# One matmul of 512 columns in place of two of 256: image and context side by side in layer 0, high and low halves side by side in layer 1

## The chip, the cores and the metric

The kernel runs on 1 core of one Trainium2 chip. The metric is device time in microseconds (us): the median of three runs of the kernel before is 2149.61 us (2144.79 to 2152.18).

## What is computed

The reference is a network of two layers on an image stream `x` of 256 tokens and a context stream `ctx` of 256 tokens, each with 2048 features, in fp32. Cut to the parts that matter:

```
mod = silu(c) @ ada_w + ada_b;  h = rmsnorm(x) * (1 + scale) + shift         # for x and for ctx
layer 0:  p = h @ e_w_in   # q, k, v, gate, a/b and four more blocks of 2048 columns
          q,k,v = silu(conv3(...)); chunked gated delta rule over 16 heads, 2 directions
          y = concat(rmsnorm(o) * silu(z), b * conv3(c*h) * silu(z_b)) @ e_w_out;  x = x + gate * y
layer 1 (image only):  u, v = gelu(h @ W);  y_c = u * (w_s @ layernorm(v) + b_s) * silu(z_c)
          y_d = (mean_r(p_d) - p_d) @ pool_w * scale * silu(z_d)
          x = x + gate * (concat(y_c, y_d) @ o_w_out);  out = rmsnorm(x)
```

In layer 0 the context is needed only for keys, values and the a/b columns; queries and everything else are computed for the image alone.

## The kernel before

Every large product is made of three: both operands are split into a high part H (rounded to the matmul's fp32r type) and a low part L (the remainder), and H.H + H.L + L.H is accumulated in PSUM. A weight chunk of 128 x 1024 is loaded (`raw`), cast to H on ACT (line 202) and subtracted to L on DVE (line 209) by `wchunk`; there are four buffers of each. `proj` (line 218) then takes 128 x 128 pieces of H and L as the stationary operand and 256 tokens of activation as the moving one: for each piece the order is H with the high activation, H with the low one, L with the high one (line 230). With two streams (`acts` of length 2) each of these is issued twice, for the image into columns 0 to 255 and for the context into columns 256 to 511 of one PSUM bank. `projT_n` (lines 236 to 241) is the other form: activations stationary, 512 weight columns moving.

The stages, in the order of time:

- **Start, 0 to 220 us.** Modulation products (`ada_cols`, line 386), normed tokens transposed and split into `hxH`, `hxL` (image) and `hcH`, `hcL` (context) by `h_cols`, and between them, on 6 weight column blocks for each of 16 rows of blocks, `k_part` (line 450), whose sums go to six tiles `kacc`.
- **Keys and values, 220 to 480 us.** Ten steps of `proj` on `wkv` for both streams, each followed by `finish` (convolution, silu, transposes); `ab_proj` (line 504) and `ab_rows` make the gate rows.
- **Head groups, 480 to 1360 us.** Four groups of four heads. In each: `wq` and `wza` products, then a chain of small products (`G`, `Q`, `E`, `PT`, `XT`, `X`, then per chunk and direction `kS`, `QS`, `z`, `Sp`, `az`, at the end `oT`), and the `wbb` products, which stand between the steps of that chain on PE as far as they reach.
- **Out of layer 0 and into layer 1, to 1563 us.** `projT` on `wout0`, the norm, `projT` on `wv1` with `h1H`, `h1L` stationary.
- **Layer 1, 1563 to 1963 us.** For four groups: `proj` on `wpz` (p half), box means on DVE, `proj` on `wpz` (z half), `proj` on `poolw` with `y1H`, `y1L` moving; then 8 blocks of `proj` on `wuz` with gelu, tanh and the token mix (`sp`, line 1138). Two PSUM tiles `pj` of two banks alternate; each is read directly by ACT and DVE.
- **`wout1`, 1963 to 2147 us.** `projT` with `y1H`, `y1L` stationary.

The order on each engine is not written out: a list scheduler with its own timeline places the instructions, and each engine then runs its queue in order. A `pj` tile can be written again when its last reader on ACT or DVE is done.

Of the kernel before, what the change touches and what calls it, by code (L numbers as in the profile page):

```python
# [17 lines left out]
P = 128  # L18
# [52 lines left out]
def layout(a):  # L71
# [34 lines left out]
    u = o[:, :D].reshape(D, 8, 256)  # L106
    z = o[:, 2 * D:3 * D].reshape(D, 8, 256)
    r["wuz"] = _blk(np.stack([u, z], 2).reshape(D, 2 * D), 512)
    p = o[:, 3 * D:4 * D].reshape(D, 4, 512)
    z = o[:, 4 * D:5 * D].reshape(D, 4, 512)  # L110
    r["wpz"] = _blk(np.stack([p, z], 2).reshape(D, 2 * D), 512)
# [4 lines left out]
    r["poolw"] = f(a["o_pool_w"][0].reshape(4, 4, P, 512).transpose(0, 2, 1, 3)).reshape(4, P, D)  # L116
# [6 lines left out]
def body(ctx: ExitStack, tc: tile.TileContext, T, dbg=None):  # L123
# [92 lines left out]

    def proj(src, cols, acts, outs, shared, kts=KT):
        nk = 1024 // cols
        for c in range(kts // nk):
            H, L = wchunk(src[:, c * 1024:(c + 1) * 1024], nk)  # L220
            for kk in range(nk):
                k = c * nk + kk
                for n, o in enumerate(outs):
# [3 lines left out]
                    m = len(acts)  # L227
# [85 lines left out]
    hxH = hxp.tile([P, KT, 256], F32R, name="hxH")  # L313
    hxL = hxp.tile([P, KT, 256], F32R, name="hxL")
# [50 lines left out]
    with ExitStack() as ph1:  # L365
        hcp = pool("hc", stack=ph1)
        hcH = hcp.tile([P, KT, 256], F32R, name="hcH")
        hcL = hcp.tile([P, KT, 256], F32R, name="hcL")

        accp = pool("acc", stack=ph1)  # L370
        with ExitStack() as ph0:
# [6 lines left out]
            acc = [accp.tile([P, 2, 512], F32, name="kacc", tag=f"kacc{b}") for b in range(6)]  # L378
# [39 lines left out]
            def norm_tok(s):  # L418
                for n in (2 * s, 2 * s + 1):
                    junk = accp.tile([P, 2, 512], F32, name="junk", tag="kacc5")  # L420
# [9 lines left out]
            def h_cols(j, srcs=(0, 1)):  # L430
                tr = gp.tile([P, 4, P], F32, name="trp", tag="g")
                for s in srcs:
                    aH, aL = ((hxH, hxL), (hcH, hcL))[s]
# [51 lines left out]
            if "hT" in dbg:  # L485
                tap("hT", hcH.bitcast(F32))
# [4 lines left out]
        def row(name):  # L491
            return ap.tile([64, 512], F32, name=name)
# [712 lines left out]
```

## Time and profile before

| what | value |
|---|---|
| median of three runs | 2149.61 us |
| the profiled execution: its time | 2155.28 us |
| its span, first to last instruction | 2153.5 us |
| PE busy (matmuls, 17034) | 2069.5 us, 96% |
| DVE busy | 1526.0 us, 71% |
| ACT busy | 999.5 us, 46% |
| DMA queues' busiest | 61.8% of 16 engines |

Busy times of PE are of pipelined instructions with modelled ends: one matmul of 256 columns is listed with 284 ns, while the next starts 120 ns after it. What a matmul costs is therefore read from the starts of neighbours in the timeline, or from a run of equal matmuls in the chain of work, never from its listed duration. The 1.8 us between time and span lie outside the first and the last instruction.

### The profile page before, as it was taken

The page shows a single profiled execution, that of the slowest core. Times are in us where ns is not written, and L with a number is a line of the kernel's source. Part 1 is how long each engine was busy: PE and PEld are TensorE (multiplying, and loading weights), DVE is VectorE, ACT ScalarE, POOL GpSimd, SP SyncE. Part 2 cuts the span into 40 slices and gives each one's busy share as a digit, 9 for nine tenths or more (in the row PEclk, how much of TensorE's full clock was granted, in tenths as well). Part 3 has the DMA queues.
Part 4 walks back from the last instruction along what each step waited for, and adds up shares of the span by engine and source line. Part 5 has one row for each costly group of instructions (what it writes and reads, how often), then busy time and mean ns, then how long its engine had stood idle before and what let it go on. Part 6 is the DMA issues. An engine that isn't in the chain of part 4 may idle for free. (4 is left out here: it accounts for less than half of the span.)

```text
span 2153.5 us, 42176 instructions
## 1 busy us (share of the span) xinstructions
PE 2069.5 (96%) x17034; PEld 1928.5 (90%) x17034; DVE 1526.0 (71%) x2715; ACT 999.5 (46%) x1728; POOL 33.8 (2%) x51
## 2 busy tenths in 40 slices
PE   6999999999999999989999999898999999999997
PEld 4789999999989999989999878677899999998886
DVE  4447987877976898489758984788687676555554
ACT  5333365225554546445645554345454444444433
POOL 0000000000000000000000000000000000000000
PEclk9999999999999999999999999999999999999999
DMA  9777655776544775366448862797866666666664
GB/s 343 263 262 243 188 182 174 238 247 233 179 134 139 247 258 179 91 225 195 133 139 258 276 187 79 253 326 260 275 219 189 180 186 197 195 187 215 192 194 131
DMA packets 151267, 446.41 MB, mean 207 GB/s; under 512 B 16512, under 2 KB 23456, under 8 KB 150048
## 3 DMA queue, kind: packets, MB, share of 16 engines
q1 hardware_dynamic: 145936, 425.37, 61.8%
q0 software_dynamic: 5136, 18.35, 2.7%
q8 instruction: 133, 2.18, 0.4%
q14 instruction: 62, 0.51, 0.1%
HBM read 423.19 MB, written 20.46 MB: 206 GB/s over the span
## 5 line engine op out<-in xcount | busy, mean ns | idle before, releaser
L209 DVE TENSOR_TENSOR L<-raw,H 128x1024 fp32r<-128x1024 f32 (+1 forms) x554 | 667.6, 1208 | 374.8 <-ACT H L202 354.1
L202 ACT CAST H<-raw 128x1024 fp32r<-128x1024 f32 (+1 forms) x554 | 574.4, 1042 | 761.7 <-PE pj L230 419.4
L230 PE MATMUL pj<-hxH,H 128*128 128x256 f32 x1856 | 528.5, 285 | 4.2 <-DVE zb L946 4.2
L230 PE MATMUL pj<-hxH,L 128*128 128x256 f32 x1856 | 527.3, 284 | 0.0
L230 PE MATMUL pj<-hxL,H 128*128 128x256 f32 x1856 | 526.8, 284 | 0.0
L230 PEld LDWEIGHTS pj<-hxH,H 128*128 128x128 f32 x1856 | 352.4, 190 | 6.3 <-DVE zb L946 4.5
L230 PEld LDWEIGHTS pj<-hxH,L 128*128 128x128 f32 x1856 | 352.4, 190 | 2.4 <-issue 1.2
L230 PEld LDWEIGHTS pj<-hxL,H 128*128 128x128 f32 x1856 | 352.4, 190 | 1.0
L230 PE MATMUL pj<-h1H,H 128*128 128x256 f32 x1024 | 290.5, 284 | 0.0
L230 PE MATMUL pj<-h1H,L 128*128 128x256 f32 x1024 | 289.8, 283 | 0.0
L230 PE MATMUL pj<-h1L,H 128*128 128x256 f32 x1024 | 289.7, 283 | 0.0
L277 DVE SCALAR_TENSOR_TENSOR acc<-araw,cs,acc 128x512 f32<-128x512 f32 x240 | 178.9, 747 | 33.0 <-DMA araw<-in_ada 20.8
L230 PEld LDWEIGHTS pj<-h1H,H 128*128 128x128 f32 x1024 | 196.5, 192 | 0.2 <-issue 0.2
L230 PEld LDWEIGHTS pj<-h1L,H 128*128 128x128 f32 x1024 | 196.5, 192 | 0.0
L230 PEld LDWEIGHTS pj<-h1H,L 128*128 128x128 f32 x1024 | 196.5, 192 | 0.0
L230 PE MATMUL pj<-hcH,L 128*128 128x256 f32 x320 | 90.4, 283 | 0.0
L230 PE MATMUL pj<-hcH,H 128*128 128x256 f32 x320 | 90.4, 282 | 0.0
L230 PE MATMUL pj<-hcL,H 128*128 128x256 f32 x320 | 90.1, 281 | 0.0
L239 PE MATMUL pj<-H,y1H 128*128 128x512 f32 x192 | 76.0, 396 | 0.0
L241 PE MATMUL pj<-H,y1L 128*128 128x512 f32 x192 | 75.9, 396 | 0.0
L240 PE MATMUL pj<-L,y1H 128*128 128x512 f32 x192 | 75.9, 395 | 0.0
L230 PEld LDWEIGHTS pj<-hcH,L 128*128 128x128 f32 x320 | 60.1, 188 | 0.5 <-issue 0.4
(428 smaller groups left out, 3659.6 us busy)
## 6 DMA issues: line engine op xcount, KB each, us to landing
raw<-in_wbb SPq DMA_DIRECT2D x128, 512.0 KB, 3.8
raw<-in_wout SPq DMA_DIRECT2D x128, 512.0 KB, 4.0
araw<-in_ada SPq DMA_DIRECT2D x192, 256.0 KB, 4.5
raw<-in_ada SPq DMA_DIRECT2D x64, 512.0 KB, 6.5
raw<-in_wpz SPq DMA_DIRECT2D x64, 512.0 KB, 3.9
raw<-in_wuz SPq DMA_DIRECT2D x64, 512.0 KB, 3.6
raw<-in_wkv SPq DMA_DIRECT2D x40, 512.0 KB, 4.7
araw<-in_ada0g SPq DMA_DIRECT2D x64, 256.0 KB, 4.5
```

The source lines that it names most:

```text
L202: S.copy(H, raw)
L209: V.tensor_tensor(L, raw, H, ALU.subtract)
L230: PE.matmul(o[:, e * 256:(e + 1) * 256] if m > 1 else o, w, a[t][:, k, :], start=st and i == 0 and e == 0, stop=sp and i == 2, skip_group_ ...
L239: PE.matmul(o, xH[:, t], H[:, kk, :], start=st, stop=False, skip_group_check=True)
L240: PE.matmul(o, xH[:, t], L[:, kk, :], start=False, stop=False, skip_group_check=True)
L241: PE.matmul(o, xL[:, t], H[:, kk, :], start=False, stop=sp, skip_group_check=True)
L277: V.scalar_tensor_tensor(aacc[u // KT], raw, cs[:, k, 0:1], aacc[u // KT], ALU.mult, ALU.add)
```

## The change

- Layer 0: one tile `hxc` [128, stream, half, 16, 256] holds image and context, high and low. `k_part` (but for row 0), the `wkv` products and the a/b product use one matmul with a moving operand of two runs of 256 columns (image, context; 32 KB apart in a partition).
- The six accumulators, `wab` and two gate rows move into one tile `acc8`, which lies in the place of the later tile `hx`. When `acc8` is done with, 8 ACT copies of 128 x 1024 bring the image half from `hxc` to `hx` (line 634), since the head groups use 256 columns as before.
- Layer 1: `h1` and `y1` hold both halves in one tile. A new function `pair` multiplies each H piece with high and low activations as 512 columns (two runs of 256, 16 KB or 32 KB apart) and each L piece with the high activations as 256; the two sums stand side by side in PSUM. ACT copies the low one to SBUF (`jn`), DVE adds the high one (`join`). A `pair` covers two blocks of 128 weight columns where `proj` covered four, so `wpz`, `poolw` and `wuz` are cut into twice as many tiles of half the size; weight chunks are as many and as large as before.
- The software DMA scratch is halved to 2048 bytes per partition.

```diff
+    def both(t, k):
+        return hxc[:, :, t, k, :]
     def proj(src, cols, acts, outs, shared, kts=KT):
...
                     for i, (w, t) in enumerate(((wH, 0), (wH, 1), (wL, 0))):
-                        for e, a in enumerate(acts):
-                            PE.matmul(o[:, e * 256:(e + 1) * 256] if m > 1 else o, w, a[t][:, k, :],
-                                      start=st and i == 0 and e == 0, stop=sp and i == 2, skip_group_check=True)
+                        PE.matmul(o, w, acts(t, k),
+                                  start=st and i == 0, stop=sp and i == 2, skip_group_check=True)
...
-    hxH = hxp.tile([P, KT, 256], F32R, name="hxH")
-    hxL = hxp.tile([P, KT, 256], F32R, name="hxL")
+    acc8 = hxp.tile([P, 8, 2, 512], F32, name="acc8", tag="hx")
...
+        hxc = hxcp.tile([P, 2, 2, KT, 256], F32R, name="hxc")
...
-                        for q in srcs:
-                            a = ((hxH, hxL), (hcH, hcL))[q]
-                            PE.matmul(ps[n][:, q * 256:(q + 1) * 256], w_, a[t][:, j, :],
-                                      start=first and i == 0 and q == 0, stop=last and i == 2, skip_group_check=True)
+                        q = slice(srcs[0], srcs[-1] + 1)
+                        PE.matmul(ps[n].rearrange("p (s t) -> p s t", s=2)[:, q], w_, hxc[:, q, t, j, :],
+                                  start=first and i == 0 and srcs[0] == 0, stop=last and i == 2, skip_group_check=True)
...
+            if step > 6:
+                for t in range(2):
+                    for q in range(1 if step < 9 else 2):
+                        k4 = slice(4 * (step - 7 + q), 4 * (step - 6 + q))
+                        S.copy(hx[:, t, k4], hxc[:, 0, t, k4])
...
+    def pair(src, x, kts=KT):
+        ps = pj.tile([P, 2, 2, 256], F32, name="pj", tag="pj")
+        for c in range(kts // 4):
+            H, L = wchunk(src[:, c * 1024:(c + 1) * 1024], 4)
+            for kk in range(4):
+                k = c * 4 + kk
+                for n in range(2):
+                    w = slice(n * P, (n + 1) * P)
+                    PE.matmul(ps[:, n], H[:, kk, w], x[:, :, k, :], start=k == 0, stop=k == kts - 1,
+                              skip_group_check=True)
+                    PE.matmul(ps[:, n, 0], L[:, kk, w], x[:, 0, k, :], start=False, stop=k == kts - 1,
+                              skip_group_check=True)
+        t = Wk.tile([P, 2, 256], F32, name="jn", tag="jn")
+        S.copy(t, ps[:, :, 1])
+        return ps[:, :, 0], t
+    def join(ps, t):
+        V.tensor_tensor(t, t, ps, ALU.add)
+        return t
...
-        ps = pj.tile([P, 4, 256], F32, name="pj", tag="pj")
-        proj(T["wpz"][2 * g + 1], 512, [(hH, hL)], [ps[:, n, :] for n in range(4)], 2)
         zs = yo
-        silu_to(zs, ps)
+        for half in range(2):
+            t = join(*pair(T["wpz"][4 * g + 2 + half], h1))
+            silu_to(zs[:, 2 * half:2 * half + 2], t)
...
-    for blk in range(8):
-        ps = pj.tile([P, 4, 256], F32, name="pj", tag="pj")
-        proj(T["wuz"][blk], 512, [(hH, hL)], [ps[:, n, :] for n in range(4)], 2)
+    for gi in range(16):
+        uz = join(*pair(T["wuz"][gi], h1))
```

Three places in the instruction order. First ACT in the `wuz` stage of layer 1, before (`ug`, `zg`: gelu and tanh of one block of 256 columns; `H<-raw`: cast of one weight chunk):

```order
L1143 ACTIVATE ug<-pj 128x256
L1064 ACTIVATE zg<-pj 128x256
L202 CAST H<-raw 128x1024
L345 CAST y1H<-ug 128x256 x2
L202 CAST H<-raw 128x1024 x7
```

The same place now (`jn<-pj`: the copy of the low sum):

```order
L202 CAST H<-raw 128x1024 x2
L1087 COPY jn<-pj 128x512
L202 CAST H<-raw 128x1024
L1171 ACTIVATE jn<-jn 128x256
L1071 ACTIVATE zg<-jn 128x256
L202 CAST H<-raw 128x1024
L348 CAST y_15705<-jn 128x256
```

Where eight casts stood between two readings of PSUM there are four, and a copy stands ahead of gelu and tanh, which now read SBUF.

Second, ACT in the stage of keys and values, now (`ct`, `cth`: convolution and tanh; `ads`: a step of the modulation sums; the row of copies has no counterpart before):

```order
L202 CAST H<-raw 128x1024
L365 ACTIVATE cth<-ct 128x512
L634 COPY hx<-hxc 128x1024 x8
L289 COPY ads<-adc 128x128
L202 CAST H<-raw 128x1024 x2
L362 ACTIVATE ct<-pj,conv_123 128x512
```

The eight copies follow each other, ahead of the next two casts of weight chunks.

Third, PE at the end of the chain of head group 1 (the second of four), before (`pj` rows are products of `wbb` that stand between the steps):

```order
L230 MATMUL pj<-hxH,H 128x256
L898 MATMUL Sp<-zk,Kt 128x128 x3
L230 MATMUL pj<-hxL,H 128x256
L898 MATMUL Sp<-zk,Kt 128x128
L230 MATMUL pj<-hxH,L 128x256
L230 MATMUL pj<-hxH,H 128x256
L909 MATMUL az<-zs,aT 128x128 x4
L867 MATMUL kS<-St,KTt 128x128 x4
L875 MATMUL QS<-St,QT 128x128 x4
```

And now, from the place where the last `pj` row of the group has gone by (the steps that follow to `oT` go on in the same way, without a `pj` row):

```order
L905 MATMUL Sp<-zk,Kt 128x128
L874 MATMUL kS<-St,KTt 128x128 x4
L882 MATMUL QS<-St,QT 128x128 x4
L905 MATMUL Sp<-zk,Kt 128x128 x3
L894 MATMUL z<-r,U 128x128 x4
L905 MATMUL Sp<-zk,Kt 128x128 x4
L916 MATMUL az<-zs,aT 128x128 x4
```

Before, `pj` products stood between these steps up to the last but one; now they have been issued earlier (62 more of them between this group's `E` and its `PT`, 815 against 753), and the last four `z` steps follow each other bare, as they do in group 3 of either kernel.

## Rows read from the trace of the kernel before

**Rows 1.** The page: span, and busy time, share of the span and instructions of PE.

```profile
span 2153.5 us, 42176 instructions
PE 2069.5 (96%) x17034; PEld 1928.5 (90%) x17034; DVE 1526.0 (71%) x2715; ACT 999.5 (46%) x1728; POOL 33.8 (2%) x51
```

**Rows 2.** What PE waited for, longest first: total us, times, longest us.

```profile
PE adm L386 <- DMA raw<-in_ada: 18.4, 3, 16.5
PE oT L926 <- DVE on L923: 13.1, 2, 6.6
PE tr L1025 <- issue: 7.7, 1, 7.7
```

**Rows 3.** The chain of work that ended last, in the `wuz` stage: start us, us, what.

```profile
1890.75 0.89 PE sp L1138 x8
1891.64 23.04 PE pj L230 x192
1914.68 0.89 PE sp L1138 x8
```

**Rows 4.** The page's groups: count, busy us and mean ns of one, idle time before.

```profile
L209 DVE TENSOR_TENSOR L<-raw,H 128x1024 fp32r<-128x1024 f32 (+1 forms) x554 | 667.6, 1208 | 374.8 <-ACT H L202 354.1
L202 ACT CAST H<-raw 128x1024 fp32r<-128x1024 f32 (+1 forms) x554 | 574.4, 1042 | 761.7 <-PE pj L230 419.4
...
L230 PE MATMUL pj<-h1H,H 128*128 128x256 f32 x1024 | 290.5, 284 | 0.0
...
L230 PE MATMUL pj<-hcH,H 128*128 128x256 f32 x320 | 90.4, 282 | 0.0
```

**Rows 5.** Smaller groups of the view by line: the same columns.

```profile
L450 PE MATMUL pj<-hcH,H 128*128 128x256 f32 x128 | 35.9, 281 | 0.0
...
L230 PE MATMUL pj<-y1H,H 128*128 128x256 f32 x64 | 18.2, 285 | 0.0
...
L450 PE MATMUL pg<-hcH,H 128*128 128x256 f32 x64 | 17.9, 280 | 0.0
```

**Rows 6.** The timeline of PE in the stage of keys and values: the first and the last of 17 neighbours, start us and listed us.

```profile
299.79 0.28 PE L230 MATMUL pj<-hxH,H 128*128 128x256 f32 x1
...
301.68 0.28 PE L230 MATMUL pj<-hxH,L 128*128 128x256 f32 x1
```

**Rows 7.** The same in the start stage: the first and the last of 23 neighbours.

```profile
153.31 0.28 PE L450 MATMUL pj<-hxH,H 128*128 128x256 f32 x1
...
155.92 0.28 PE L450 MATMUL pj<-hxH,L 128*128 128x256 f32 x1
```

**Rows 8.** The same in the `wout1` stage, 512 columns: the first and the last of 13 neighbours.

```profile
2000.12 0.40 PE L241 MATMUL pj<-H,y1L 128*128 128x512 f32 x1
...
2002.92 0.40 PE L241 MATMUL pj<-H,y1L 128*128 128x512 f32 x1
```

**Rows 9.** The same in the `wv1` stage, 512 columns with `h1` as the stationary operand: the first and the last of 16 neighbours.

```profile
1519.59 0.39 PE L239 MATMUL pj<-H,h1H 128*128 128x512 f32 x1
...
1522.99 0.39 PE L239 MATMUL pj<-H,h1H 128*128 128x512 f32 x1
```

**Rows 10.** The timeline of PE in head group 0: a matmul of 512 columns whose moving operand is four runs of the same 128 columns, and the next.

```profile
532.14 0.39 PE L753 MATMUL E<-mneg,identr 128*128 128x512 f32 x1
532.38 0.28 PE L230 MATMUL pj<-hxH,L 128*128 128x256 f32 x1
```

**Rows 11.** Stretches of 50 us: busy us (instructions) of PE, PEld, DVE, ACT, POOL; granted clock, DMA share, GB/s.

```profile
200.00:250.00 50.00, 50.00 (x425) 50.00 (x424) 46.36 (x66) 12.11 (x15) 0.00 (x0) 1.00 0.68 209
250.00:300.00 50.00, 50.00 (x427) 50.00 (x426) 48.21 (x119) 34.42 (x101) 0.00 (x0) 1.00 0.47 153
...
1600.00:1650.00 50.00, 50.00 (x424) 49.67 (x424) 38.56 (x64) 22.48 (x30) 3.75 (x7) 1.00 0.67 211
...
1900.00:1950.00 50.00, 50.00 (x420) 50.00 (x419) 27.90 (x37) 21.22 (x29) 1.07 (x2) 1.00 0.62 182
```

**Rows 12.** The timeline of PE at the end of head group 1: start us, listed us, and in brackets the idle time before and what ended it.

```profile
928.35 1.26 PE L887 MATMUL z<-r,U 128*128 128x128 f32 x8 [0.72 <-DVE r L870]
930.34 1.16 PE L909 MATMUL az<-zs,aT 128*128 128x128 f32 x8 [0.73 <-ACT zs L894]
938.07 1.94 PE L926 MATMUL oT<-cst,on 128*128 128x128 f32 x8 [6.57 <-DVE on L923]
```

**Rows 13.** The same at the end of head group 3, whose last steps have no products between them.

```profile
1332.25 1.26 PE L887 MATMUL z<-r,U 128*128 128x128 f32 x8 [0.22 <-DVE r L870]
1335.34 2.08 PE L898 MATMUL Sp<-zk,Kt 128*128 128x128 f32 x8 [1.82 <-ACT zk L891]
...
1342.25 1.26 PE L898 MATMUL Sp<-zk,Kt 128*128 128x128 f32 x8 [0.59 <-ACT zk L891]
...
1348.07 1.16 PE L909 MATMUL az<-zs,aT 128*128 128x128 f32 x8 [0.73 <-ACT zs L894]
...
1352.63 1.16 PE L909 MATMUL az<-zs,aT 128*128 128x128 f32 x8 [0.73 <-ACT zs L894]
1360.36 1.94 PE L926 MATMUL oT<-cst,on 128*128 128x128 f32 x8 [6.57 <-DVE on L923]
```

**Rows 14.** The tile `kacc`: duration ns min/median/max of a DVE addition and an ACT copy that read 512 columns of PSUM.

```profile
L483 DVE TENSOR_TENSOR kacc<-kacc,pg x16: 678/681/689, 55.5 to 220.8; 128x512 f32<-128x512 f32 x16
...
L481 ACT COPY kacc<-pg x4: 580/596/610, 34.4 to 42.7; 128x512 f32<-128x512 f32 x4
```

More of the change, by code (lines that the diff above doesn't have):

```diff
@@ L365, in body @@
     with ExitStack() as ph1:
[L366 to L370, printed above, removed]
+        hxcp = pool("hxc", stack=ph1, side="right")
+        hxc = hxcp.tile([P, 2, 2, KT, 256], F32R, name="hxc")
         with ExitStack() as ph0:
@@ L377, in body @@
             k0r = pool("k0r", 3, stack=ph0)
-            acc = [accp.tile([P, 2, 512], F32, name="kacc", tag=f"kacc{b}") for b in range(6)]
+            acc = [acc8[:, b] for b in range(6)]
             def ada_cols(j):
@@ L485, in body @@
             if "hT" in dbg:
-                tap("hT", hcH.bitcast(F32))
+                tap("hT", hxc[:, 1, 0].bitcast(F32))
         ap = pool("abp", stack=ph1)
@@ L502, in ab_proj @@
                     for t in range(2):
-                        for e, a in enumerate(((hxH, hxL), (hcH, hcL))):
-                            PE.matmul(abp[:, 256 * e:256 * e + 256], wHL[:, k, :], a[t][:, k, :],
-                                      start=k == 0 and t == 0 and e == 0, stop=k == KT - 1 and t == 1,
-                                      skip_group_check=True)
+                        PE.matmul(abp.rearrange("p (s t) -> p s t", s=2), wHL[:, k, :], both(t, k),
+                                  start=k == 0 and t == 0, stop=k == KT - 1 and t == 1, skip_group_check=True)
                 ab, abl = row("ab"), row("a_")
@@ L622, in body @@
             ps = pj.tile([P, 2, 512], F32, name="pj", tag="pj")
-            proj(T["wkv"][b // 4, b // 2 % 2, b % 2], 256, [(hxH, hxL), (hcH, hcL)], [ps[:, 0, :], ps[:, 1, :]], 1)
+            proj(T["wkv"][b // 4, b // 2 % 2, b % 2], 256, both, [ps[:, n, :].rearrange("p (s t) -> p s t", s=2) for n in range(2)], 1)
             if early:
@@ L700, in body @@
             ps = pj.tile([P, 4, 256], F32, name="pj", tag="pj")
-            proj(T["wq"][grp], 512, [(hxH, hxL)], [ps[:, n, :] for n in range(4)], 2)
+            proj(T["wq"][grp], 512, one(hxH, hxL), [ps[:, n, :] for n in range(4)], 2)
             for i in range(3):
@@ L724, in body @@
             ps = pj.tile([P, 4, 256], F32, name="pj", tag="pj")
-            proj(T["wza"][grp], 512, [(hxH, hxL)], [ps[:, n, :] for n in range(4)], 2)
+            proj(T["wza"][grp], 512, one(hxH, hxL), [ps[:, n, :] for n in range(4)], 2)
             for i in range(3):
@@ L934, in body @@
                 ps = pj.tile([P, 4, 256], F32, name="pj", tag="pj")
-                proj(T["wbb"][j], 512, [(hxH, hxL)], [ps[:, n, :] for n in range(4)], 2)
+                proj(T["wbb"][j], 512, one(hxH, hxL), [ps[:, n, :] for n in range(4)], 2)
                 cg = B.tile([P, 256], F32, name="cg", tag="ct")
@@ L992, in body @@
     H1 = pool("h1")
-    hH = H1.tile([P, KT, 256], F32R, name="h1H")
-    hL = H1.tile([P, KT, 256], F32R, name="h1L")
+    h1 = H1.tile([P, 2, KT, 256], F32R, name="h1")
+    hH, hL = h1[:, 0], h1[:, 1]
     Wo = pool("wo", 2)
@@ new lines, in body @@
+    for gi in range(16):
+        uz = join(*pair(T["wuz"][gi], h1))
+        if gi % 2 == 0:
+            blk = gi // 2
+            wsT = Wk.tile([P, 2, P], F32, name="wsT", tag="wsT")
+            qdma(wsT.rearrange("p g q -> p (g q)"), T["wsT"][:, blk * 256:(blk + 1) * 256])
+            bsb = Wk.tile([P, 2, P], F32, name="bsb", tag="bsb")
+            qdma(bsb.rearrange("p g q -> p (g q)"), T["bs"][:, blk * 256:(blk + 1) * 256].partition_broadcast(P))
+        n = gi % 2
+        sp = gp.tile([P, 2, P], F32, name="sp", tag="g")
+        for c in range(2):
+            PE.matmul(sp[:, c, :], v[c][:, gi * P:(gi + 1) * P], wsT[:, n, :], start=True, stop=True)
+        st = Wk.tile([P, 2, P], F32, name="st", tag="st")
+        V.tensor_tensor(st, sp, bsb[:, n:n + 1, :].to_broadcast([P, 2, P]), ALU.add)
+        st = st.rearrange("p a b -> p (a b)")
+        ug = uz[:, 0]
+        S.activation(ug, ug, AF.Gelu_apprx_tanh)
+        zg = Wk.tile([P, 256], F32, name="zg", tag="zg")
+        silu_to(zg, uz[:, 1])
+        V.tensor_tensor(ug, ug, st, ALU.mult)
+        V.scalar_tensor_tensor(ug, zg, 0.5, ug, ALU.mult, ALU.mult)
+        split(yH[:, gi, :], yL[:, gi, :], ug)
```

65 lines of the change are left out of this document (26 added, 39 removed).

## Prediction

> **What bounds the kernel now.** I read the page first: PE is listed as busy for 96% of the span [rows 1]. Listed times overlap, so I then read what PE waited for. The three longest entries come to 39 us of 2153.5, and 16.5 us of these are one wait at the start [rows 2]. So PE's queue is nearly always full, and the question is what one product costs it. The last chain shows that best: in the `wuz` stage 192 products of 256 columns take 23.04 us between two `sp` steps, with nothing in between, which is 120.0 ns each [rows 3]. In the stage of keys and values 16 intervals take 1.89 us, 118.1 ns each [rows 6]; in the start stage 22 take 2.61 us, 118.6 ns [rows 7]. Products of 512 columns start 233.3 ns apart in `wout1` (12 intervals in 2.80 us) [rows 8] and 226.7 ns apart in `wv1` (15 in 3.40 us) [rows 9]. The clock is granted in full, 2.4 GHz, in the stretches looked at [rows 11]. Two narrow products thus cost 236 to 240 ns, one wide one 227 to 233: a small part of each product does not depend on its columns, and the change pays it once instead of twice.
>
> **What is merged.** The counts come from the groups. Layer 1 has 1024 products of each of the three kinds on `h1` [rows 4] and 64 on `y1` [rows 5]: 1088 triples. A triple takes 3 x 120.0 = 360.0 ns and becomes a wide product and a narrow one. The narrow one is as before, 120.0. With a wide one at 233.3 the triple loses 6.7 ns, in all 7.3 us; at 226.7 it loses 13.3 ns, 14.5 us. Keys and values: 320 of each kind on `hcH` [rows 4], so 960 pairs of 236.2 ns; at 233.3 they lose 2.9 ns each, 2.8 us, at 226.7 9.5 ns, 9.1 us. Start: 128 + 64 = 192 of each kind [rows 5], 576 pairs, less 36 of row 0 that stay apart, so 540 of 237.2 ns: 2.1 us or 5.7 us. The a/b product, 32 pairs: 0.1 or 0.3 us. **Sum: 12.3 to 29.6 us.**
>
> Of these ends I take 226.7 for layer 1, since that row is of the same `h1` and the same weight buffers, and 233.3 for layer 0, for which no row of 512 columns uses its tiles: 14.5 + 2.8 + 2.1 + 0.1 = 19.5 us. That the moving operand now has two runs should cost nothing: one of four runs of 128 has the next product start 0.24 us later, as the plain ones do [rows 10].
>
> **What is added in layer 1.** There are 16 + 16 + 8 = 40 pairs. Each adds a copy of 512 PSUM columns on ACT, 0.60 us, and an addition on DVE of 512, 0.68 us, or two smaller ones [rows 14]: 24 us and 27 us. ACT is busy for 21 to 22 of 50 us there and DVE for 28 to 39 [rows 11], so over the stage of 400 us both fit. The full pairs take 16 x 2 x 347 ns = 11.1 us on PE, and the tile that one of them frees is wanted only when the next has run, so copy and addition (1.28 us) are hidden even behind a cast (1.04) and a split (1.21) [rows 4]. The eight `poolw` pairs are short, 8 x 347 ns = 2.8 us, and the same chain with both ahead of it is 3.5 us: uncovered, 0.7 us each, 5.6 us. I take 0, as the order has the weight chunks for them converted earlier, and keep 5.6 us for the range.
>
> **What is added in layer 0.** The eight copies to `hx` are 8 x 1.04 = 8.3 us in one piece on ACT [rows 4]. Behind them stand casts of weight chunks. A chunk there is 24 wide products, 5.6 us of PE, and four buffers let the casts run ahead by up to three further chunks, 17 us; ACT has 16 to 38 us of 50 free there [rows 11]. I take 0; the price, if nothing covers it, is 8.3 us. DVE is nearer to its limit: 46.4 and 48.2 of 50 us busy in two stretches [rows 11]. A faster PE needs the splits sooner; if DVE sets the pace in these 100 us, their share of the gain is lost, 100 us / 236.2 ns = 423 pairs x 2.9 ns = 1.2 us. I take 1.
>
> **What is moved.** The order changes in many places, by the scheduler's hand. The one that leaves PE without cover is the end of head group 1: its `wbb` products are issued before the chain, and the last four `z` steps stand bare. Group 3 shows the same row of steps bare: from its `z` at 1332.25 to `oT` at 1360.36 are 28.1 us [rows 13], in which 16 sets of 8 small products need 16 x 0.89 = 14.2 us [rows 3], so 13.9 us are idle. Group 1 has 8.7 us of idle time in its bare end: 9.7 us from `z` to `oT` less two sets, and 0.7 before [rows 12]. The difference is 5.2 us; by the idle times alone, 10.7 against 8.0, it is 2.7 us [rows 12, 13]. I take 4 us. The products themselves are not lost, they ran earlier.
>
> The halved DMA scratch serves the loads on POOL's queue, for which PE's longest waits show no entry [rows 2]: 0.
>
> **The sum.** 19.5 - 4 - 1 = 14.5 us. The profiled execution, 2155.3 us (span 2153.5), would become 2140.8. It lies 5.7 us above the median of the runs, 2149.6, so I predict **2135 us** as the median. All gains at their upper end and no cost: 2149.6 - 29.6 = 2120. All at their lower end with every cost of the range (5.2, 1.2, 5.6): 2149.6 - 12.3 + 12.0 = 2149.3.
>
> **The rivals.** First, **columns alone set the price**: a wide product costs two narrow ones of 118.1 ns, 236.2. Then only layer 1 gains, 3.8 ns a triple, 4.1 us, which the bare end of group 1 takes back: 2149.6. For it: the costs per column differ by only 3 to 5%, and narrow products of 118.1 and 120.0 ns stand beside each other unexplained [rows 3, 6]. Against it: 226.7 and 233.3 ns are rows, steady over 12 and 15 intervals [rows 8, 9]. The Trainium skill has a rule near this rival ("TensorE: Matmul & The Clock Gate", section "Back-to-back issue gap"): a product takes its columns at 2.4 GHz plus about 2.5 ns. By it a merge saves 2.5 ns and 2620 merges 6.6 us, an estimate from that page, and the time would be some 2148. The trace speaks against it: narrow products stand 118 to 120 ns apart where the rule gives 109, wide ones 227 to 233 where it gives 216, so more than 2.5 ns is fixed per product.
>
> Second, **slower: ACT's queue stands behind the copy.** The copy of a pair waits for PE's last product, and whatever cast stands behind it cannot go. If less than one chunk (2.8 us of PE) is converted ahead at that moment, PE starts each next pair only after a cast and a split, 1.04 + 1.21 = 2.25 us [rows 4]. At the 32 full pairs that is 72 us, with the gains about 2149.6 - 14.5 + 72 = 2207. For it: before, ACT's longest wait was already the cast on PE's `pj`, 419.4 us in all [rows 4], so casts come just in time for a free buffer. Against it: four buffers are free to run ahead, and in the order casts stand right ahead of each copy. It turns the sign when about 7 of the 32 pairs are hit.
>
> Third, **the short pairs and the `hx` copies are uncovered**, 5.6 + 8.3 us: the gain is then 19.5 - 5 - 13.9 = 0.6 us, 2149.
>
> **How the numbers follow.** The forecast gets 0.70, price by columns 0.13, uncovered pieces 0.09, the slower rival 0.08. About 0.3%, 6.4 us, is what a measurement of this kernel can tell from no change, so faster means below 2143.2 and slower above 2156.0. The forecast's own spread is 2120 to 2145, nearly all of it faster: 0.71 with a little from the others. The two rivals near 2149 make most of the 0.20 for no change, the second rival the 0.09 for slower. The range 2120 to 2150 holds the forecast and both rivals near 2149 and leaves out the slower one and a small part above the upper bound of the gain.
>
> **What the profile after would show.** In the `wuz` stage 32 wide and 32 narrow products should take 11.1 us (11.3 at 233.3) between two `sp` steps, where half a block took 11.52; wide products in keys and values should start 227 to 233 ns apart, and start and keys and values together end some 5 us earlier. Head group 1 should show waits of 0.6 to 1.8 us at `z`, `Sp` and `az` ahead of its `oT`. No wait of PE on the copy or the addition should stand in its list. I am wrong if wide products stand 236 ns or more apart, if PE waits on casts at the starts of pairs, or if the head groups, whose code the change leaves alone, move by more than the 4 us.

## The result and the profile after

The changed kernel takes **2136.96 us** (median of 6 runs, 2133.69 to 2140.87) where the kernel before takes 2149.57 (6 runs, 2144.79 to 2152.18). The ratio is 0.995 with a 95% interval of 0.9936 to 0.9964, so 7.7 to 13.8 us less. Forecast were 2135 us, within 2120 to 2150. The total is right; the two largest terms behind it are not, as the profile shows.

The page of the changed kernel: span and PE's row, to be set beside [rows 1]. PE has 2620 instructions fewer, one for each merge, and its share of the span is the same.

```profile
span 2139.1 us, 37062 instructions
...
PE 2053.8 (96%) x14414; PEld 1787.5 (84%) x14414; DVE 1546.8 (72%) x2767; ACT 1024.2 (48%) x1764; POOL 33.9 (2%) x51
```

What PE waited for, beside [rows 2] (total us, times, longest us). The three long ones are still there. New is a wait of `sp` for the transfer of its weights `wsT`.

```profile
PE adm L387 <- DMA raw<-in_ada: 17.1, 3, 16.5
PE oT L933 <- DVE on L930: 13.1, 2, 6.6
PE tr L1032 <- issue: 10.7, 1, 10.7
...
PE sp L1166 <- DMA wsT<-in_wsT: 3.5, 1, 3.5
```

The chain in the `wuz` stage, beside [rows 3]: three neighbouring `sp` steps.

```profile
1867.76 0.45 PE sp L1166 x4
...
1879.50 0.44 PE sp L1166 x4
...
1891.05 0.45 PE sp L1166 x4
```

From the second to the third are 11.55 us, of which `sp` takes 0.45. The 32 wide and 32 narrow products of a pair thus take 11.10 us, as forecast (11.1), where half a block took 11.52. So do the other five pairs after this one. From the first to the second are 11.74 us, and the products take 11.30, the forecast's figure for the dearer wide product; the pair ahead of it takes as long.

Keys and values, beside [rows 6]: the first and the last of 20 neighbouring wide products.

```profile
299.21 0.39 PE L234 MATMUL pj<-hxc,H 128*128 128x512 f32 x1
...
303.66 0.40 PE L234 MATMUL pj<-hxc,L 128*128 128x512 f32 x1
```

That is 19 intervals in 4.45 us, 234.2 ns each, where two narrow ones took 236.2 [rows 6]. Now whole stages, in a view of stretches with the columns of [rows 11]. First the kernel before: keys and values from their first to their last product; the head groups, from there to the first product of layer 0's output that reads `ybH` (which stands ahead of the end of group 3's chain); the products of layer 1, from the first `wpz` to the last `wuz` product.

```profile
227.10:473.00 245.90, 245.90 (x2106) 243.79 (x2105) 202.56 (x421) 107.35 (x251) 0.00 (x0) 1.00 0.62 196
...
473.00:1210.50 737.50, 711.20 (x7014) 697.91 (x7012) 576.74 (x1138) 395.17 (x777) 9.16 (x12) 0.97 0.60 190
1563.10:1962.20 399.10, 399.10 (x3341) 398.25 (x3340) 261.57 (x390) 178.54 (x241) 11.79 (x22) 1.00 0.64 192
```

The same three stretches of the changed kernel:

```profile
224.80:467.50 242.70, 242.70 (x1142) 195.49 (x1141) 206.55 (x430) 114.91 (x258) 0.92 (x1) 1.00 0.66 213
...
467.50:1194.20 726.70, 708.52 (x7016) 695.09 (x7014) 576.46 (x1139) 395.78 (x777) 8.26 (x11) 0.99 0.61 191
1548.10:1948.50 400.40, 393.80 (x2257) 342.92 (x2257) 288.02 (x446) 196.82 (x271) 11.80 (x22) 0.99 0.61 191
```

The first number after each stretch is its length. Keys and values are 3.2 us shorter, the head groups, which the change leaves alone, 10.8 us shorter, and layer 1, for which 14.5 us of gain were forecast, is 1.3 us *longer* in these two executions. Layer 1 has a place where PE stands. The timeline of PE at group 0's `poolw` products (in brackets the idle time and what ended it):

```profile
1597.86 0.51 PE L1082 MATMUL pj<-y,H 128*128 128x512 f32 x1 [0.55 <-DVE jn L1091]
...
1603.05 0.68 PE L1166 MATMUL sp<-wsT,v 128*128 128x128 f32 x4 [3.53 <-DMA wsT<-in_wsT]
...
1610.62 0.50 PE L1082 MATMUL pj<-h,H 128*128 128x512 f32 x1 [2.08 <-DVE jn L1091]
```

The scheduler put six `sp` steps, of the first three `wuz` blocks, between these products, and `wsT` has two buffers. It also interleaved the two `poolw` pairs of this group: PE runs 8 products of the first, 8 of the second and then, twice, 4 of each, where groups 1 to 3 have 16 and then 16. The chain of work that ended last shows what this leads to:

```profile
1596.72 6.18 DMA wsT<-in_wsT
1603.05 0.68 PE sp L1166 x4
...
1607.66 1.06 ACT H L202
1608.75 0.54 DVE L L209
...
1609.89 0.69 DVE jn L1091
1610.62 0.50 PE pj L1082
```

After the wait for `wsT` it goes over a cast of a weight chunk on ACT, which stood 9.2 us for PE and starts as the last wide product of the first pair ends, and over the split of that chunk on DVE, behind which the pair's join is queued. The granted clock around it:

```profile
1597.00:1604.00 7.00, 2.92 (x18) 2.27 (x18) 4.16 (x10) 0.64 (x1) 2.40 (x5) 1.00 0.80 245
1604.50:1607.50 3.00, 3.00 (x12) 2.61 (x12) 1.29 (x2) 0.00 (x0) 0.54 (x1) 0.50 0.05 15
1608.00:1611.00 3.00, 0.92 (x6) 0.56 (x5) 2.25 (x3) 2.62 (x4) 0.13 (x1) 1.00 0.52 138
1611.50:1614.50 3.00, 3.00 (x11) 2.61 (x10) 2.64 (x7) 0.00 (x0) 0.00 (x0) 0.50 0.79 250
1615.00:1618.00 3.00, 3.00 (x19) 2.63 (x18) 1.75 (x2) 2.01 (x3) 0.00 (x0) 1.00 0.08 31
```

After the wait for `wsT` and after the one for the second join stands a stretch at 0.50, the lower level of 1.2 GHz, in which PE is busy throughout and issues 11 or 12 products where the last row, at the full clock, has 19. The three waits sum to 6.2 us, and the half clock adds to them.

### The profile page after: what moved, and what is told of

It is laid out like the page before. It is cut to its first block, busy times and chain, and to the rows that moved or that the text cites. A ratio compares the mean times of both kernels' runs of the same rounds, so it can differ in the third digit from the quotient of the medians.

```text
span 2139.1 us, 37062 instructions
## 1 busy us (share of the span) xinstructions
PE 2053.8 (96%) x14414; PEld 1787.5 (84%) x14414; DVE 1546.8 (72%) x2767; ACT 1024.2 (48%) x1764; POOL 33.9 (2%) x51
## 5 line engine op out<-in xcount | busy, mean ns | idle before, releaser
L234 PE MATMUL pj<-hx,H 128*128 128x256 f32 x3072 | 566.5, 284 | 0.0
L234 PEld LDWEIGHTS pj<-hx,H 128*128 128x128 f32 x3072 | 478.7, 190 | 3.3 <-issue 0.6
L234 PE MATMUL pj<-hx,L 128*128 128x256 f32 x1536 | 436.3, 284 | 0.0
L1082 PE MATMUL pj<-h,H 128*128 128x512 f32 x1024 | 361.8, 397 | 2.1 <-DVE jn L1091 2.1
L234 PEld LDWEIGHTS pj<-hx,L 128*128 128x128 f32 x1536 | 291.8, 190 | 2.1 <-issue 1.0
L1084 PE MATMUL pj<-h,L 128*128 128x256 f32 x1024 | 288.1, 281 | 0.0
L1082 PEld LDWEIGHTS pj<-h,H 128*128 128x128 f32 x1024 | 192.7, 188 | 47.5 <-DVE jn L1091 2.4
L234 PE MATMUL pj<-hxc,H 128*128 128x512 f32 x640 | 205.0, 399 | 0.0
L281 DVE SCALAR_TENSOR_TENSOR acc<-araw,cs,acc 128x512 f32<-128x512 f32 x240 | 178.8, 746 | 22.8 <-DMA araw<-in_ada 10.8
L1084 PEld LDWEIGHTS pj<-h,L 128*128 128x128 f32 x1024 | 194.2, 190 | 0.2 <-issue 0.2
L234 PEld LDWEIGHTS pj<-hxc,H 128*128 128x128 f32 x640 | 119.5, 188 | 28.2 <-issue 0.8
L450 PEld LDWEIGHTS pj<-hxc,H 128*128 128x128 f32 x272 | 49.8, 193 | 14.4 <-issue 4.5
```

The lines of the kernel that those rows point to most:

```text
L234: PE.matmul(o, w, acts(t, k), start=st and i == 0, stop=sp and i == 2, skip_group_check=True)
L281: V.scalar_tensor_tensor(aacc[u // KT], raw, cs[:, k, 0:1], aacc[u // KT], ALU.mult, ALU.add)
L450: PE.matmul(ps[n].rearrange("p (s t) -> p s t", s=2)[:, q], w_, hxc[:, q, t, j, :], start=first and i == 0 and srcs[0] == 0, stop=last and ...
L1082: PE.matmul(ps[:, n], H[:, kk, w], x[:, :, k, :], start=k == 0, stop=k == kts - 1, skip_group_check=True)
L1084: PE.matmul(ps[:, n, 0], L[:, kk, w], x[:, 0, k, :], start=False, stop=k == kts - 1, skip_group_check=True)
```

## Experiments

The theory before the runs: merging pays 2 to 3 ns a pair in layer 0 and about 10 ns a triple in layer 1; layer 1's share is lost at the wait for `wsT`; the head groups' share comes from the new order and tiles. The rival for layer 1 was PSUM handed back late by the joins of the short `poolw` pairs. Medians of the kernel before in the four sets of runs were 2148.55, 2145.65, 2146.73 and 2146.69 us, so results of different sets are compared by their ratios to it. Each diff is against the changed kernel, unless another is named.

**Layer 0 alone.** Layer 1 and its weight layout are those of before.

```diff
...
+        proj(T["wpz"][2 * g], 512, one(hH, hL), [ps[:, n, :] for n in range(4)], 2)
...
-                ps, lo = pair(T["wpz"][4 * g + n // 2], h1)
...
```

> The change in layer 0 alone (layer 1 and its weights as before; the halved scratch stays). Theory, from the two traces: layer 0 up to the first product of its output carries the whole gain, 16.3 us, and layer 1 gives none, so 2149.6 - 16 = about 2133, range 2128 to 2139, a little below the changed kernel's 2137. Rival, the prediction's own terms (start -2.1, keys and values -2.8 + 1, head group 1 +4, so about 0 in layer 0): 2149, range 2146 to 2152, with the whole gain in layer 1.

Measured: 2139.21 us (12 runs), ratio 0.9963, interval 0.9951 to 0.9975: 8.0 us less (5.4 to 10.5). Between the two expectations: layer 0 does carry most of the gain, but half of what the two traces had said.

**Layer 1 alone.**

```diff
-    def both(t, k):
-        return hxc[:, :, t, k, :]
...
+            proj(T["wkv"][b // 4, b // 2 % 2, b % 2], 256, [(hxH, hxL), (hcH, hcL)], [ps[:, 0, :], ps[:, 1, :]], 1)
...
```

> The change in layer 1 alone (layer 0 as before; the scratch is halved, since the wider tiles need the room). Theory: its triples run at about 350 ns in place of 360 (11 us less), and a stall of TensorE on the third block's sp product, with the half clock behind it, gives 11 to 13 us back: 2150, range 2146 to 2154. Rival, the prediction's term (14.5 us less and nothing given back): 2135, range 2132 to 2139.

Measured: 2147.27 us (12 runs), ratio 0.9999, interval 0.9985 to 1.0013. Layer 1 as the change has it gives nothing that the runs can tell (3.2 us less to 2.8 more). Its layer 0 has the order of the kernel before, so its trace is a second execution of it: its head groups take 731.4 us, not 737.5. A part of the 10.8 us is the luck of one execution. So is a part of layer 1's 400.4: here the same order, with waits of 3.3, 2.2 and 0.6 us at the same place, takes 396.6 (the granted clock is the third number from the end).

```profile
1554.90:1951.50 396.60, 390.05 (x2258) 341.50 (x2257) 288.16 (x446) 196.94 (x271) 11.83 (x22) 1.00 0.62 193
```

**The halved scratch alone**, on the kernel before.

```diff
-    nc = bacc.Bacc("TRN2", target_bir_lowering=False, num_devices=1, dynamic_dma_scratch_size=4096)
+    nc = bacc.Bacc("TRN2", target_bir_lowering=False, num_devices=1, dynamic_dma_scratch_size=2048)
```

> The kernel before with the halved scratch and nothing else; the order of every engine is that of the kernel before. Theory: no change, 2148.5, range 2146 to 2151, and the head groups from the last key/value product to the first product with the output weights take 731 to 738 us as in the two profiles of that order so far. Rival (the halved scratch holds up POOL's transfers): 2 us or more slower.

Measured: 2146.73 us (12 runs), ratio 1.0005, interval 0.9992 to 1.0018: no cost, as forecast. Its head groups take 728.0 us, shorter than the 731 to 738 that I expected of the same order.

**Layer 0 with narrow products**, all else as changed.

```diff
-                        PE.matmul(o, w, acts(t, k),
-                                  start=st and i == 0, stop=sp and i == 2, skip_group_check=True)
+                        xs = acts(t, k)
+                        for e, x in enumerate(xs):
+                            PE.matmul(o[:, e] if len(xs) > 1 else o, w, x,
+                                      start=st and i == 0 and e == 0, stop=sp and i == 2, skip_group_check=True)
...
```

> The changed kernel, its tiles, its copies and its layer 1, but with every layer-0 product of 512 columns over image and context issued as two of 256 again (start, keys and values, a and b). Theory 1 (merging pays its 2 to 3 ns a pair in the start and in keys and values, 5.5 us, and the head groups' 10.8 us come from the tiles and not from the merging): 2137 + 5.5 = 2142, range 2139 to 2146. Theory 2 (the head groups' 10.8 us hang on the order that the scheduler makes from the wide products): 2153, range 2149 to 2157. Since the order of VectorE's instructions around the heads differs from that of the changed kernel, a time between or outside the two says that the head groups' time moves with the order by itself.

Measured: 2143.24 us (11 runs), ratio 0.9977, interval 0.9966 to 0.9988, against 0.995: undoing the merges costs 5.8 us, near theory 1's 5.5. Keys and values take 246.0 us as before. The head groups stay short with narrow products, though in an order of their own, so it is not the merging that shortens them:

```profile
472.40:1196.80 724.40, 702.73 (x7015) 690.38 (x7013) 575.26 (x1137) 396.41 (x777) 8.29 (x11) 0.99 0.60 191
```

**Three `wsT` tiles** in the changed kernel.

```diff
-            wsT = Wk.tile([P, 2, P], F32, name="wsT", tag="wsT")
+            wsT = Wk.tile([P, 2, P], F32, name="wsT", tag="wsT", bufs=3)
...
-        st = Wk.tile([P, 2, P], F32, name="st", tag="st")
+        st = Wk.tile([P, 2, P], F32, name="st", tag="st", bufs=1)
```

> The changed kernel with three wsT tiles in place of two, and one st tile in place of two to pay for the room (st is written and read by VectorE alone). The sp steps of blocks 0 to 2 that stand between group 0's poolw products then find their weights in place. Theory: the wait of 3.5 us on the wsT transfer and the half clock behind it go, 10 to 13 us, so 2137 - 11 = about 2126, range 2122 to 2130. Rival A (layer 1 loses in the hand-back of the short poolw pairs' PSUM, the wait on jn, and in the copies): no change, 2137, range 2134 to 2139. Rival B (the clock falls at this place whatever the wait): 3.5 us less, 2133.

Measured: 2135.62 us (5 runs), ratio 0.9948, interval 0.9933 to 0.9964: no change that can be told from 0.995. The theory falls. The wait for `wsT` is gone, and PE now waits at the same place for the join:

```profile
1602.33 0.80 PE L1082 MATMUL pj<-h,H 128*128 128x512 f32 x1 [4.34 <-DVE jn L1091]
```

The timeline of DVE of the same kernel says why the join (L1091) is late:

```profile
1599.25 1.29 DVE L1152 TENSOR_TENSOR v<-v,lnb 128x512 f32<-128x512 f32 x2 [3.18 <-DMA lnb<-in_lnb]
...
1601.60 0.68 DVE L1091 TENSOR_TENSOR jn<-jn,pj 128x512 f32<-128x512 f32 x1
```

DVE stands 3.18 us for `lnb`, the shift of the token mix's layer norm, whose one buffer is reloaded for each of four pieces, and the join is queued behind it. The changed kernel has this wait too, 3.79 us; there it ran beside the wait for `wsT` and was over before the pair was complete. DVE then stood idle until the cast came, with the split and the join behind it:

```profile
1608.75 1.23 DVE L209 TENSOR_TENSOR L<-raw,H 128x1024 fp32r<-128x1024 f32 x1 [2.50 <-ACT H L202]
1609.89 0.68 DVE L1091 TENSOR_TENSOR jn<-jn,pj 128x512 f32<-128x512 f32 x1
```

So several waits lay side by side, and the visible one hid the others. PE's waits in layer 1 sum to 6.2 us with two `wsT` tiles and to 4.9 with three.

**Scale and shift in two buffers**, eight pieces of 256 columns, first without and then with the three `wsT` tiles.

```diff
-    for e in range(4):
-        es = slice(e * 512, (e + 1) * 512)
-        lnw = Wk.tile([P, 512], F32, name="lnw", tag="lnw", bufs=1)
+    for e in range(8):
+        es = slice(e * 256, (e + 1) * 256)
+        ln = Wk.tile([P, 2, 256], F32, name="ln", tag="ln", bufs=2)
...
```

> The changed kernel with the scale and shift of the token mix's layer norm loaded in eight pieces of 256 columns into two buffers, in place of four pieces of 512 into one (same room, everything else as it is; with this the scheduler puts the sp steps of two blocks between group 0's poolw products, not of three). Theory, after the run with three wsT tiles lost its wsT wait and got a wait of 4.3 us on jn in its place: VectorE stands 3.2 to 3.8 us for lnb's transfer with the pair's join queued behind it, and TensorE runs out of PSUM because a poolw pair is only 2.8 us of work. With the next piece already there, both waits and the half clock behind them go: 2135.6 - 4.3 - 3.4 = about 2128, range 2124 to 2131. Rival: the poolw pairs are too short for VectorE's other work at this place (L copies, joins), so a wait on jn of the same length stays: 2134 to 2137.

> Both edits: scale and shift in two buffers, and three wsT tiles. Theory: 2128, the same as with the two buffers for scale and shift alone, since there the third block's sp is not in this place. If the wsT wait has a price of its own, this run is 3 us or more below the other.

Measured: 2134.73 us (6 runs; ratio 0.9946, 0.9927 to 0.9965) and 2135.12 us (6 runs; 0.9945, 0.9926 to 0.9964). The rival holds. DVE in the first of the two still stands for the pieces, in shorter waits:

```profile
1597.35 0.76 DVE L1150 TENSOR_TENSOR v<-v,ln 128x256 f32<-128x256 f32 x2 [1.55 <-DMA ln<-in_lnw]
...
1602.21 0.76 DVE L1150 TENSOR_TENSOR v<-v,ln 128x256 f32<-128x256 f32 x2 [2.83 <-DMA ln<-in_lnw]
...
1604.69 0.68 DVE L1091 TENSOR_TENSOR jn<-jn,pj 128x512 f32<-128x512 f32 x1
```

and PE's wait for the join is 6.04 us at 1605.42; with three `wsT` tiles as well, the longest is 5.6. The wait for `wsT` has no price of its own here. Two buffers did not get the pieces there ahead of DVE; why the transfers come that late is not shown.

**Without the reloads**, with three `wsT` tiles. The kernel leaves out six of the eight loads of scale and shift, so its result is not the reference's.

```diff
-        lnw = Wk.tile([P, 512], F32, name="lnw", tag="lnw", bufs=1)
-        qdma(lnw, T["lnw"][:, es].partition_broadcast(P))
...
+        if e == 0:
+            lnw = Wk.tile([P, 512], F32, name="lnw", tag="lnw", bufs=1)
+            qdma(lnw, T["lnw"][:, es].partition_broadcast(P))
...
```

> The kernel with three wsT tiles, and the layer norm of the token mix takes the scale and shift of its first 512 columns for all four pieces: six of the eight loads are left out, the arithmetic on VectorE stays. Theory (the transfers of scale and shift hold VectorE, and with it the joins, in both earlier runs): no wait on jn and no half clock at group 0, layer 1 from its first branch product to its last u/z product takes about 389 us in place of 400, the run 2126, range 2122 to 2130. Rival (the 2.8 us of a poolw pair are too short for VectorE's own work there, transfers or not): a wait on jn of 2 us or more stays, 2132 to 2136.

Measured: 2132.86 us (6 runs), ratio 0.9932, interval 0.9918 to 0.9945; layer 1 takes 395.3 us, with the reloads and three `wsT` tiles 396.6. The rival holds: with the transfers gone PE still waits 4 us for two joins:

```profile
1598.18 0.50 PE L1082 MATMUL pj<-y,H 128*128 128x512 f32 x1 [1.82 <-DVE jn L1091]
...
1605.58 0.50 PE L1082 MATMUL pj<-h,H 128*128 128x512 f32 x1 [2.23 <-DVE jn L1091]
```

Ahead of the first of these joins DVE is busy without a break from 1585.8 us on, first with the scaling and then with splits and box means. Ahead of the second it is not; it stands for a cast:

```profile
1603.70 1.23 DVE L209 TENSOR_TENSOR L<-raw,H 128x1024 fp32r<-128x1024 f32 x1 [3.12 <-ACT H L202]
1604.84 0.68 DVE L1091 TENSOR_TENSOR jn<-jn,pj 128x512 f32<-128x512 f32 x1
```

The scaling has been over since 1590.6 there. So the transfers are a part of the wait, not its cause, and DVE's own work on the scaling isn't the whole of it either: the chain of cast, split and join is left, behind two pairs that are interleaved here too (8, 8 and then, twice, 4 and 4).

**The scaling late**, behind group 3's joins, in the changed kernel, and then with layer 1 alone changed.

```diff
-        t = Wk.tile([P, 2, 256], F32, name="jn", tag="jn")
+        t = Wk.tile([P, 2, 256], F32, name="jn", tag="jn", bufs=4)
...
-        lnw = Wk.tile([P, 512], F32, name="lnw", tag="lnw", bufs=1)
+        lnw = Wk.tile([P, 512], F32, name="lnw", tag="jn", bufs=4)
...
-        lnb = Wk.tile([P, 512], F32, name="lnb", tag="lnb", bufs=1)
+        lnb = Wk.tile([P, 512], F32, name="lnb", tag="jn", bufs=4)
...
-            fw = Wk.tile([P, 512], F32, name="fw", tag=("lnw", "lnb")[e], bufs=1)
+            fw = Wk.tile([P, 512], F32, name="fw", tag="jn", bufs=4)
```

> The changed kernel with the tiles of scale and shift taken from the rotation of the join tiles jn (four buffers in place of two, for the room of lnw and lnb), nothing left out. The rotation puts the scaling behind the joins of group 3, where a u/z pair is 11.2 us of work, in place of group 0. Theory: the waits at group 0 go and a pair of 11 us hides the same transfers: 2126, range 2122 to 2131. Rival: the wait comes back between group 3's two poolw joins, 2133 to 2137.

> The change in layer 1 alone (layer 0 as before) with the same edit to the scaling. Theory: layer 1's merging pays its 10.9 us once group 0's wait is gone, 2147 - 10 = 2137, range 2133 to 2141. Rival (the pairs lose elsewhere what the wide products gain): 2145 to 2149, as without the edit.

Measured: **2130.05 us** (6 runs), ratio 0.9913, interval 0.9898 to 0.9928, and 2135.29 us (6 runs), ratio 0.9939, interval 0.9923 to 0.9954. Both theories hold. This is the best version, below both kernels, and is called the late kernel from here on. In its order the scaling stands behind group 3's joins (1753 to 1773 us in its trace), and the `poolw` pairs of group 0 follow one another, 16 products and then 16. The edit also gives `jn` four buffers in place of two; no run has any of these three alone. Layer 1 of the first, as a stretch, beside 400.40 of the changed kernel:

```profile
1546.60:1937.30 390.70, 390.26 (x2258) 340.43 (x2257) 288.40 (x446) 197.03 (x271) 12.88 (x24) 1.00 0.61 197
```

PE stands for 0.4 us in it, at the full clock. And both stretches of the second, whose layer 0 has the order of before:

```profile
472.00:1199.60 727.60, 706.10 (x7013) 692.70 (x7011) 576.14 (x1138) 395.07 (x777) 9.18 (x12) 0.99 0.59 192
1548.40:1938.90 390.50, 390.06 (x2258) 340.48 (x2258) 288.52 (x446) 196.95 (x271) 12.87 (x24) 1.00 0.61 197
```

**Narrow products in layer 1**, in the changed kernel and in the one with the late scaling.

```diff
-                    PE.matmul(ps[:, n], H[:, kk, w], x[:, :, k, :], start=k == 0, stop=k == kts - 1,
-                              skip_group_check=True)
+                    for t in range(2):
+                        PE.matmul(ps[:, n, t], H[:, kk, w], x[:, t, k, :], start=k == 0 and t == 0,
+                                  stop=k == kts - 1, skip_group_check=True)
```

> The changed kernel with each 512-column product of layer 1 issued as two of 256 again (high and low apart); pairs, joins, copies, tiles and weights' layout stay. Theory: 1088 triples go from 350 to 360 ns, 10.9 us, and the wait at group 0 stays: 2137 + 11 = 2148, range 2145 to 2151. Rival A (columns alone set the price of a product, 2.5 ns a merge): 2137 + 2.7 = 2140. Rival B (the wait at group 0 is hidden by the slower products): 2140 to 2143.

> The kernel with the late scaling, and each 512-column product of layer 1 issued as two of 256 (high and low apart): the price of the merging in layer 1 with no wait at group 0 in either. Theory (a triple takes 350 ns wide and 360 narrow): 1088 x 10 ns, 2130 + 11 = 2141, range 2138 to 2144, and the 45 us from 1650 on hold PE fully busy in both. Rival (the columns alone set the time, 2.5 ns a merge): 2130 + 2.7 = 2133, range 2130 to 2136.

Measured: 2144.91 us (12 runs), ratio 0.9997, interval 0.9983 to 1.0011, and 2139.14 us (12 runs), ratio 0.9968, interval 0.9957 to 0.9979. Against their wide twins that is 10.1 us (0.9997 less 0.995) and 9.1 us by the medians, 11.8 by the ratios: the theory's 11, not the 2.7 of the price by columns. In the late kernel layer 1 takes, with narrow products:

```profile
1542.50:1942.90 400.40, 400.12 (x3346) 398.84 (x3345) 289.17 (x446) 196.97 (x271) 12.88 (x24) 1.00 0.60 193
```

9.7 us more than wide, with PE busy throughout in both. In the first of the two layer 1 takes 404.3 us, so with narrow products the waits at group 0 cost 3.9, where the wide order loses 6.1 to 9.7 to them, by the execution (396.6 against 390.5, 400.4 against 390.7): the second rival was right to that extent. The granted clock with narrow products stays full there (1.00 from 1600 to 1650 us).

## Why the prediction was right in the sum and wrong in its steps

**The price of a merge: right in kind.** The forecast that something in each product does not depend on its columns holds: 1088 merges of layer 1 are worth 9.1 to 11.8 us. The first rival, price by columns, falls. The rule that the Trainium skill gives for an isolated product ("TensorE: Matmul & The Clock Gate", section "Back-to-back issue gap") is not met either: its 2.5 ns a merge would be 2.7 us there, an estimate from that page. What the fixed part consists of stays open: every merge takes away a weight load as well as a product (PEld's count falls with PE's, from 17034 to 14414), and no run separates the two.

**Layer 1's term, -14.5: failed.** Measured: 0.2 us less by the run with layer 1 alone (3.2 less to 2.8 more). By the traces it was too large for the layer as a whole: without any wait, it goes from 399.1 to 390.7 us, 8.4 less; and with narrow products in the new pairs it is at 400.4, so the pairs by themselves cost 1.3 and the merging gives 9.7. The forecast took 226.7 ns for every wide product, a triple of 346.7. In the late kernel's trace about half of the triples, now a wide and a narrow product, start 347 ns after the one before, a third 350 and one in seven 361, no less than the 360 of three narrow products; why, stays open. The runs alone are less strict: layer 1 with the late scaling is 13.1 us less (9.9 to 16.5), more than the 8.6 of its stage, and the rest stands in no stage that the change touches. In the kernel as changed all of it was given back, by the runs.

**The copies and joins of layer 1 at 0, with 5.6 us as the price of the short pairs: failed**, and this is the larger error. The mechanism was in the prediction: a cast and a split ahead of copy and addition, 3.5 us in all, against the 2.8 us of a short pair. It took 0 because the order was to have the weight chunks converted earlier. At group 0 neither the 2.8 us nor the early chunks are there. Since its two pairs are interleaved, both PSUM tiles and both weight chunks are held to the end. The next cast starts only as the first pair ends (1607.66 us), the first pair's tile is free at 1610.62, and of the 3.0 us between them only the last 4 products of the second pair, some 0.7 us, are covered. Where DVE is free at that moment, the wait is 2.1 to 2.2 us (changed kernel and run without the reloads); where it stands for the scaling's transfers, 4.3 and 6.0. The wait for `wsT` and DVE's work on the scaling ahead of the other join come on top.

In the three traces whose layer 1 has the changed kernel's order and products that costs 9.7 us (400.4 against the late 390.7), 6.1 (396.6, with layer 1 alone) and 6.6 (397.3, with narrow products in layer 0); by the ratios of the runs 8.0 (0.995 against 0.9913) and 12.9 (0.9999 against 0.9939). That moving the scaling away removes the waits is shown by these runs. That it does so because DVE's box means then come early enough for the scheduler to issue the pairs one after the other is argued, since no run changes the order of the pairs alone. My first reading, the wait for `wsT`, was the visible part. The kernel before has the same scaling at the same place, and PE has no wait in that stretch; there a group's `poolw` products are one tile of 48 narrow ones, 5.8 us at 120 ns, and there is no second tile to interleave.

**Keys and values, -2.8 + 1: right.** The stage went from 245.9 to 242.7 us, -3.2 where -1.8 was forecast, in every profile with wide products, and stood at 246.0 with narrow ones. No loss to DVE is seen in it. **Start, -2.1: open.** The last product of the key part lies at 217.9 to 219.3 us in four profiles of before's order and at 217.1 to 218.8 in nine of the changed order, 0.5 less on average, within their spread. Together with the narrow run, 5.8 us for all merges of layer 0 against 5.0 forecast.

**Head groups, +4: failed, also in sign.** The waits at group 1's bare end came, but smaller than forecast: the listed ones sum to 9.1 us where they were 8.0 [rows 12], 1.1 more and not 4.

```profile
900.84 1.26 PE L905 MATMUL Sp<-zk,Kt 128*128 128x128 f32 x8 [0.52 <-ACT zk L898]
906.74 1.26 PE L905 MATMUL Sp<-zk,Kt 128*128 128x128 f32 x8 [0.52 <-ACT zk L898]
912.56 1.16 PE L916 MATMUL az<-zs,aT 128*128 128x128 f32 x8 [0.73 <-ACT zs L901]
917.13 1.16 PE L916 MATMUL az<-zs,aT 128*128 128x128 f32 x8 [0.73 <-ACT zs L901]
924.86 1.51 PE L933 MATMUL oT<-cst,on 128*128 128x128 f32 x6 [6.57 <-DVE on L930]
```

But the new order also has no counterpart to other waits. In the trace of before, DVE stood for a transfer of the modulation's weights, with `kvT` queued behind it, and PE stood for `kvT`; later PE stood for `zb`. First DVE, then PE:

```profile
484.29 0.75 DVE L277 SCALAR_TENSOR_TENSOR acc<-araw,cs,acc 128x512 f32<-128x512 f32 x1 [3.35 <-DMA araw<-in_ada]
```

```profile
487.98 0.63 PE L599 MATMUL kvp<-cst,kvT 128*128 128x128 f32 x4 [1.92 <-DVE kvT L363]
...
773.51 0.58 PE L230 MATMUL pj<-hxH,H 128*128 128x256 f32 x1 [3.38 <-DVE zb L946]
```

The wait for `kvT` is not the order's own: two other traces of the same order have it at 0.4 us or not at all. The one for `zb` is, 3.3 to 4.2 us in all four traces of the order of before and absent in the nine of the changed one. I had counted the end that got worse and not looked for those that got better. Over the profiles the head groups take 737.5, 731.4, 728.0 and 727.6 us in the order of before (731.1 on average) and 722.2 to 726.7 in nine of the changed order (725.1): 6 us less, of which the next stretch, up to `tr`, gives 2 back (it goes from 251.5 to 253.4 us on average). A part of the 6 is the clock: the two traces of before's order with a granted clock of 0.99 take 728.0 and 727.6, less than 3 us above the changed order's mean. That the waits are the cause of the rest is argued from the traces. Narrow products keep the head groups short, at 724.4 us, with a wait of 2.6 us for `zb` and 0.2 for `kvT`, so the merging is not the cause; what of it is the tiles, the copies to `hx` or the scheduler's order stays open, since no run changed these singly. A move of the head groups by more than 4 us was one of the prediction's own signs of being wrong, and it was the sign that spoke.

**The copies to `hx` and the scratch at 0: right.** No wait stands at them, and the scratch alone gives 1.0005. **The slower rival**, casts held up behind the copy at all 32 full pairs, did not come: PE's waits at pairs are at group 0 alone. There it is the other way round, the copy stands behind a cast that waits for PE.

So 14.5 us were forecast from layer 1 and about 0 from layer 0, its own gains eaten up by the heads. Measured alone, layer 0 gives 8.0 us (5.4 to 10.5) and layer 1 0.2 (3.2 less to 2.8 more). Two errors of 8 to 14 us nearly cancelled. That the time came out right is luck, and it was no proof of the reasons.

## What to carry to other kernels

Merging two products over the same weights saves the part of each that its columns don't set (here 8 to 11 ns each in layer 1, some 3 in keys and values), but it also halves the work behind which the tile's reader must finish: look for the short tile whose reader has other work queued ahead, and move that work to where a tile is long. Look too at the order in which the short tiles are filled: two that are filled in turns are full at the same time, and then hardly anything covers the reader of the first. When a wait is removed and the time stays, look at the same microsecond for the wait that it hid. And take a second trace of the unchanged kernel before explaining a difference of 10 us in a part that the change leaves alone.

## What the hardware showed that was not expected

A wait can cost more than its length through the granted clock, and it varies by execution: in the changed kernel's trace the waits of 3.5 and 2.1 us at group 0 were each followed by a stretch at 1.2 GHz with PE fully busy. With layer 1 alone, the same order had waits of 3.3 and 2.2 us, and only the first was followed by one (granted clock 0.52 from 1610.5 to 1613.5 us, 1.00 from 1617.5 to 1620.5). Executions of one order differ by as much as the change is worth: in the four traces with the head groups' order of before, that stage's mean granted clock is 0.97 where it takes 737.5 us and 0.99 where it takes 727.6, and PE is busy for 711.2 and 706.1 us of it with the same instructions. A wide product over the same operands does not always start the same time after its neighbour either: triples stand 347, 350 and 361 ns apart in one trace, all at the full clock.
